# An encoder kernel: the sync engine's transfers in the order of the program

## The chip, the cores and the metric

The kernel runs on one core of one Trainium2 chip. A core has five engines with a queue of instructions each: TensorE (PE in the profile; PEld is its weight load), VectorE (DVE), ScalarE (ACT), GpSimd (POOL) and SyncE (SP). SP computes nothing here: it issues DMA transfers between HBM and the core's SBUF, one after the other, and an instruction in its queue that has to wait holds up all that stand behind it. The metric is the device time of one execution in microseconds (us).

## The reference

One layer of a bidirectional encoder on two sequences, 1024 and 256 tokens of 1024 features, in float32. After a norm, one projection feeds a Fourier mixing branch and a six-head latent attention; their outputs are joined and projected (`w_out`), then comes a SwiGLU feed-forward block with 2816 hidden units, and a last norm.

```python
def trunk(x):
    x = x + token_mixer(rms_norm(x, norm_mix_g), w_in, q_norm_g, w_q_up, kv_norm_g, w_kv_up, w_out)
    x = x + (silu(rms_norm(x, g) @ w_gate) * (rms_norm(x, g) @ w_up)) @ w_down
    return rms_norm(x, final_norm_g)
```

## The kernel before

**Arithmetic.** Each float32 operand is split into two parts, a rounded "hi" part and the rest "lo", and `mm3` (line 100) makes a product out of three: hi by hi, hi by lo, lo by hi. A weight therefore goes through four hands: SP loads it raw (`wload`, line 136, or `load_w`), ACT copies the hi part (line 93), POOL or DVE subtracts to get the lo part (line 98), and only then can TensorE use all of it. The raw weights share a pool of four buffers (`wraw`); a further load waits until POOL or DVE has read the oldest of them.

**Stages.** The token axis is cut into chunks of 512, 512 and 256 (`TC`). In order of time: the input projection, with the loads of `x` (`load_x`) and `w_in` (`load_w`); the query projections, whose results go to HBM through `q_rope` (line 589) and come back through `qload` (lines 695 and 697); the attention blocks (`Block`), in which the exponentials are turned by small transfers (`move`, line 808) and the row sums are stored (`inverse`, line 795) and read back spread out (`spread`, line 800); the output projection `out_proj`, which stores its result to `hd` (line 1106); the gate and up projections (`run`, `rest`, `prep`), eleven units of 256 hidden columns each, whose results go to HBM through `put` (line 1249); and the down projection (`down`), which reads them back by `load_a` (lines 1407 and 1409, five transfers a unit) and takes `w_down` through the class `Weights` (line 138). `load_h` (lines 1444, 1446) fetches the residual for the sum.

**What sets the order.** The kernel is written for a tile framework whose scheduler decides the order of each engine's queue. `tc.manual_schedule` names the engines whose queue keeps the order of the program instead: PE, ACT, DVE and POOL. SP is not among them, so the scheduler places SP's transfers by its own plan, and a load whose buffer is free may be put ahead of a store that the program issues earlier. Waits for data and for buffers are added by the framework.

**Around the two seams that matter below.** After the last attention head has started its last block, the program calls `inverse` for head 5, chunk 1 (a store of the row sums on SP that waits for DVE), and then `W.split(io + 2)`, which loads and splits the first two pieces of `w_out`:

```python
at(first[n] + 4, lambda: W.split(io + 2))
```

At the end of the gate and up stage the program goes through the last unit's `put`s, and then:

```python
load_a(0)
for t in range(3):
    split_a(0, t)
W.end = len(wspec)
W.split(idn + 2)
load_a(1)
```

`load_a(0)` reads what unit 0 left in HBM far earlier; `W.split(idn + 2)` loads four pieces of `w_down` and splits two. The down projection then runs units of two hidden tiles (`fp`) over three token chunks and eight output tiles (`m`); a group `down((fp,), m, t)` is 12 matmuls for a chunk of 512. PSUM has four buffers (`mm`) for these groups.

Of the kernel before, what the change touches and what calls it, by code (L numbers as in the profile page):

```python
# [35 lines left out]
def encoder_kernel(ctx, tc, A, out):  # L36
# [5 lines left out]
                mybir.EngineType.Activation,  # L42
                mybir.EngineType.DVE,
                mybir.EngineType.Pool,
            }
        )
    )
# [1595 lines left out]
```

## Time and profile before

| | |
|---|---|
| median of 3 runs | 1452.13 us (1449.49 to 1455.31) |
| the profiled execution, whole | 1450.82 us |
| its span, first to last instruction | 1449.0 us |
| DVE busy | 851.4 us (59%) |
| ACT busy | 548.7 us (38%) |
| POOL busy | 616.8 us (43%) |
| transfers on the hardware queue of SP (q1) | 150.74 MB, 34.0% of the 16 DMA engines' time |
| mean granted TensorE clock | 0.988 |

How to read it: times in the timeline are microseconds from the first instruction; a row of the timeline is a run of like instructions on one engine, with its start, its length and, in brackets, the idle time of the engine ahead of it and what ended that. `SPq` marks the issue of a transfer, not its flight; an `SPq` row is long when its later transfers had to wait.

### The profile page before, as it was taken

Reading aid. Unit: us, or ns where it says so; the run is one execution under the profiler, and the core shown is the slowest. Engines: PE = TensorE matmul, PEld = TensorE weight load, DVE = VectorE, ACT = ScalarE, POOL = GpSimd, SP = SyncE. Lnnn points to the kernel's source line nnn. Section 1 sums busy time; section 2 is a strip of 40 time slices with the busy share of each in tenths; the row PEclk is TensorE's granted clock in tenths of the full one; section 3 lists DMA queues with packets and bytes.
Section 4 is the critical chain, followed back from the end, with each engine's and each line's share of the span. In section 5 each row is a group of like instructions: output and inputs, shape, how many; then the busy total and the mean of one; then the engine's idle time right before and its main releaser. Section 6 shows DMA issues by size and latency. Waiting matters only on the chain.

```text
span 1449.0 us, 27553 instructions
## 1 busy us (share of the span) xinstructions
PE 1396.8 (96%) x11096; PEld 1350.2 (93%) x11096; DVE 851.4 (59%) x1291; ACT 548.7 (38%) x1107; POOL 616.8 (43%) x444
## 2 busy tenths in 40 slices
PE   9999998999989997899999999999999999999997
PEld 8999897888869997899999999999999999999996
DVE  6778668898993765954234324332432466777434
ACT  5554446676763424432222222222223332113133
POOL 3466524453542644264444444444353142334333
PEclk9999999999999998999999999999999999999998
DMA  7103445686765652031212121212222542234002
GB/s 256 58 1 121 148 131 141 154 203 152 198 187 145 205 159 75 16 110 66 65 60 95 57 69 67 95 49 73 70 84 89 174 164 89 85 128 161 1 37 110
DMA packets 76192, 157.50 MB, mean 109 GB/s; under 512 B 13216, under 2 KB 23200, under 8 KB 75936
## 3 DMA queue, kind: packets, MB, share of 16 engines
q1 hardware_dynamic: 73008, 150.74, 34.0%
q10 hardware_dynamic: 2736, 3.95, 0.8%
q8 instruction: 87, 1.43, 0.4%
q0 software_dynamic: 320, 1.05, 0.2%
q14 instruction: 41, 0.34, 0.1%
HBM read 99.57 MB, written 35.16 MB: 93 GB/s over the span
## 4 chain that ended last, share of the span: by engine, by line
PE 78%; DVE 10%; issue 3%; ACT 3%; POOL 2%; DMA 1%; SPq 0%; ACTq 0%; DVEq 0%; POOLq 0%
PE mm L112 49%; PE sc L112 22%; PE sc L747 1%; PE sc L748 1%; PE sc L751 1%; PE sc L750 1%; PE sc L749 1%; DVE mx L758 1%; DVE b L98 1%; DVE mx L98 1%; PE mm L824 1%; DVE c L1114 1%; POOL wo L98 0%; DVE at L98 0%; DVE wraw L818 0%
## 5 line engine op out<-in xcount | busy, mean ns | idle before, releaser
L112 PE MATMUL mm<-at,whl 128*128 128x256 f32 x2640 | 304.6, 278 | 4.2 <-DVE h L1437 2.3
L112 PEld LDWEIGHTS mm<-at,whl 128*128 128x128 f32 x2640 | 302.7, 189 | 5.4 <-DVE h L1437 2.9
L112 PE MATMUL sc<-b,wo 128*128 128x256 f32 x2288 | 291.2, 278 | 4.7 <-ACT wo L93 2.5
L112 PEld LDWEIGHTS sc<-b,wo 128*128 128x128 f32 x2288 | 275.0, 189 | 5.3 <-ACT wo L93 3.5
L98 POOL TENSOR_TENSOR wo<-wraw,wo 128x512 fp32r<-128x512 f32 x148 | 200.7, 1379 | 164.7 <-ACT wo L93 164.7
L1257 DVE TENSOR_TENSOR e<-e,sc 128x512 f32<-128x512 f32 x64 | 43.9, 688 | 225.6 <-PE sc L112 225.6
L1437 DVE TENSOR_TENSOR h<-h,mm 128x512 f32<-128x512 f32 (+1 forms) x192 | 111.8, 596 | 103.2 <-PE mm L112 102.6
L98 POOL TENSOR_TENSOR whl<-wraw,whl 128x1024 fp32r<-128x1024 f32 (+3 forms) x49 | 117.3, 2410 | 85.4 <-ACT whl L93 78.4
L112 PE MATMUL mm<-hn,wo 128*128 128x256 f32 x1056 | 130.7, 277 | 0.0
L112 PE MATMUL mm<-b,wo 128*128 128x256 f32 x1056 | 127.1, 276 | 0.7 <-ACT b L93 0.5
L112 PEld LDWEIGHTS mm<-hn,wo 128*128 128x128 f32 x1056 | 125.5, 188 | 0.0
L112 PEld LDWEIGHTS mm<-b,wo 128*128 128x128 f32 x1056 | 123.1, 188 | 1.1 <-ACT b L93 0.7
L112 PEld LDWEIGHTS mm<-mx,whl 128*128 128x128 f32 x960 | 114.3, 191 | 2.2 <-POOL whl L98 1.5
L112 PE MATMUL mm<-mx,whl 128*128 128x256 f32 x960 | 115.0, 281 | 1.1 <-POOL whl L98 0.9
L93 ACT ACTIVATE at<-araw 128x512 fp32r<-128x512 f32 x55 | 32.8, 624 | 160.0 <-DMA araw<-a 106.7
L93 ACT ACTIVATE wo<-wraw 128x512 fp32r<-128x512 f32 x156 | 87.8, 619 | 4.3 <-PE mm L112 2.0
L112 PE MATMUL mm<-pt,vt 128*128 128x512 f32 (+1 forms) x324 | 83.1, 391 | 6.2 <-DVE pt L98 5.8
L98 POOL TENSOR_TENSOR wo<-tmp,wo 128x512 fp32r<-128x512 f32 x22 | 29.3, 1335 | 137.7 <-ACT wo L93 137.7
L1450 POOL TENSOR_TENSOR h<-h,araw 128x512 f32<-128x512 f32 (+1 forms) x24 | 27.5, 1151 | 136.6 <-DVE h L1437 84.7
L98 POOL TENSOR_TENSOR pt<-wraw,pt 128x512 fp32r<-128x512 f32 x40 | 60.6, 1514 | 52.6 <-ACT pt L93 46.8
L1085 POOL TENSOR_TENSOR hacc<-hacc,tmp 128x512 f32<-128x512 f32 (+1 forms) x35 | 42.2, 1205 | 86.5 <-ACT tmp L1084 80.3
L112 PEld LDWEIGHTS mm<-pt,vt 128*128 128x128 f32 x324 | 57.2, 191 | 19.3 <-DVE pt L98 7.6
(199 smaller groups left out, 2269.7 us busy)
## 6 DMA issues: line engine op xcount, KB each, us to landing
Y<-P SPq DMA_DIRECT2D x160, 128.0 KB, 2.6
wraw<-in_w_gate SPq DMA_DIRECT2D x22, 512.0 KB, 4.2
wraw<-in_w_up SPq DMA_DIRECT2D x22, 512.0 KB, 4.3
wraw<-in_w_down SPq DMA_DIRECT2D x22, 512.0 KB, 3.5
araw<-a SPq DMA_DIRECT2D x44, 256.0 KB, 4.4
a<-e SPq DMA_DIRECT2D x42, 256.0 KB, 2.0
araw<-in_x SPq DMA_DIRECT2D x32, 256.0 KB, 4.4
wraw<-in_w_out SPq DMA_DIRECT2D x16, 512.0 KB, 4.0
```

Of the source, the lines that this page charges most:

```text
L93: nc.scalar.activation(o, i, AF.Copy)
L98: eng.tensor_tensor(o, i, f(hi), op=ALU.subtract)
L112: nc.tensor.matmul(o[:, c], L[a], R[b][:, c], start=first and i == 0 and j == 0, stop=end, skip_group_check=again)
L747: nc.tensor.matmul(o, qn[0][:, cs], k[0], start=True, stop=False)
L748: nc.tensor.matmul(o, qn[0][:, cs], k[1], start=False, stop=False)
L749: nc.tensor.matmul(o, qn[1][:, cs], k[0], start=False, stop=False)
L750: nc.tensor.matmul(o, qr[0][:, cs], krst[kt], start=False, stop=False)
L751: nc.tensor.matmul(o, qr[1][:, cs], krst[kt], start=False, stop=True)
L1085: nc.gpsimd.tensor_tensor(acc[t], acc[t], q, op=ALU.add)
L1257: add = lambda o, x, y: nc.vector.tensor_tensor(o, x, y, op=ALU.add)
L1437: nc.vector.tensor_tensor(hview(m, t), hview(m, t), o, op=ALU.add)
L1450: nc.gpsimd.tensor_tensor(HV[m, t], HV[m, t], hres.pop((m, t)), op=ALU.add)
```

## The change

SP joins the engines whose queue keeps the program's order. No transfer is added, taken away or resized, and the order of the four other engines stays what it was.

```diff
@@ -42,6 +42,7 @@
                 mybir.EngineType.Activation,
                 mybir.EngineType.DVE,
                 mybir.EngineType.Pool,
+                mybir.EngineType.SP,
             }
         )
     )
```

## The prediction

> **What bounds the kernel now.** I read the page's head first, then the timeline of SP against the order in which the source issues transfers, and then, at each place where the two differ, the engine that waits for the transfer.
>
> ```profile
> span 1449.0 us, 27553 instructions
> ...
> PE 1396.8 (96%) x11096; PEld 1350.2 (93%) x11096; DVE 851.4 (59%) x1291; ACT 548.7 (38%) x1107; POOL 616.8 (43%) x444
> ...
> L112 PE MATMUL mm<-at,whl 128*128 128x256 f32 x2640 | 304.6, 278 | 4.2 <-DVE h L1437 2.3
> ```
>
> TensorE is busy for 1396.8 of 1449.0 us, so at most 52 us can be won anywhere, and a transfer matters only where its lateness reaches TensorE. The third row is the down projection: TensorE stood idle ahead of it for 4.2 us in all. Now SP's queue where that stage begins:
>
> ```profile
> 1083.35 1.58 SPq L138 DMA_DIRECT2D wraw<-in_w_down  x2
> ...
> 1103.12 1.75 SPq L1407 DMA_DIRECT2D araw<-a  x4
> ...
> 1107.96 1.58 SPq L138 DMA_DIRECT2D wraw<-in_w_down  x2
> ...
> 1116.99 10.68 SPq L1249 DMA_DIRECT2D a<-e  x4
> ...
> 1128.74 0.32 SPq L1249 DMA_DIRECT2D b<-tmp  x1
> 1129.15 1.83 SPq L1407 DMA_DIRECT2D araw<-a  x4
> ...
> 1131.88 9.63 SPq L138 DMA_DIRECT2D wraw<-in_w_down  x4
> ```
>
> In the program the last unit's five `put`s (line 1249) come first, then `load_a(0)`, then four `w_down` loads, then `load_a(1)`. SP's own order is different: two `w_down` loads run 33 us ahead of those stores, `load_a(0)` 14 us, the next two `w_down` 9 us. That is a prefetch over the seam, and the change takes it away. The same kind of lead stands in four other places.
>
> **The change, part by part.** It adds and removes no instruction: it only moves transfers in one queue. Each load moves back behind the stores written ahead of it.
>
> *1. The seam to the down projection.* What the prefetch buys:
>
> ```profile
> 1108.40 2.72 ACT L93 ACTIVATE at<-araw 128x512 fp32r<-128x512 f32 x5
> ...
> 1111.03 1.99 ACT L93 ACTIVATE whl<-wraw 128x1024 fp32r<-128x1024 f32 x2
> ...
> 1112.15 4.75 POOL L98 TENSOR_TENSOR whl<-wraw,whl 128x1024 fp32r<-128x1024 f32 x2 [2.96 <-ACT whl L93]
> ...
> 1127.10 0.39 PE L112 MATMUL mm<-at,whl 128*128 128x256 f32 x2
> ...
> 1129.37 20.86 PE L112 MATMUL mm<-at,whl 128*128 128x256 f32 x167 [1.89 <-DVE at L98]
> ...
> 1131.93 0.63 ACT L93 ACTIVATE at<-araw 128x512 fp32r<-128x512 f32 x1 [18.91 <-DMA araw<-a]
> ...
> 1134.24 0.63 ACT L93 ACTIVATE at<-araw 128x512 fp32r<-128x512 f32 x1 [1.68 <-DMA araw<-a]
> ```
>
> Both weights were split by 1116.9, while TensorE still worked on the unit before, and it lost 1.89 us. Afterwards the last store, which waits for the stage's last result, still goes at 1128.74, and only then comes `load_a(0)`. Before, exactly there, stood `load_a(1)` and two `w_down` loads of the same sizes, so their flight is the measure; the rows are the issue views of 1129.1 to 1131.3 and of 1131.5 to 1133:
>
> ```profile
> araw<-a SPq DMA_DIRECT2D x4, 256.0 KB, 3.6
> araw<-b SPq DMA_DIRECT2D x1, 256.0 KB, 5.3
> ...
> wraw<-in_w_down SPq DMA_DIRECT2D x2, 512.0 KB, 6.2
> ```
>
> ACT got the first `a` at 1131.93 and the third at 1134.24; the fifth, `b`, issued at 1131.1, landed 5.3 later at 1136.4, ahead of the weights. The two `w_down`, issued at 1131.88 and 0.4 later, landed 6.2 us on in the median, the pair about 1.2 apart: 1137.7 and 1138.9. The hi copies (1.99 / 2 = 1.0 each) end at 1138.7 and 1139.9, POOL's lo parts (4.75 / 2 = 2.4 each, one after the other) at 1141.1 and 1143.5. The first group of 12 matmuls ends with those that need the second lo part: 1143.5 + 2 x 0.125 (20.86 / 167) = 1143.75. Before, two of the twelve had run and the other ten ended at 1129.37 + 10 x 0.125 = 1130.6. Loss: **13.1 us**, all of it on TensorE. Behind it nothing else is late: `load_a(1)` comes four 512 KB loads later, about 5 us, and the four PSUM buffers let TensorE run on for four groups (6 us) without DVE.
>
> The bounds: if the second lo part could be hidden, 2.4 less (10.7); if the flights of 6.2 grew by a half because more loads are queued at once, 3.1 more (16.2).
>
> A long gap also costs clock. The windows view (length; busy PE, PEld, DVE, ACT, POOL; granted clock; DMA):
>
> ```profile
> 561.00:570.00 9.00, 0.28 (x1) 0.28 (x1) 1.45 (x3) 1.59 (x3) 7.77 (x7) 0.65 0.08 29
> 570.00:572.00 2.00, 2.00 (x7) 1.47 (x8) 2.00 (x4) 1.75 (x4) 0.00 (x0) 0.50 0.00 0
> ...
> 574.00:576.00 2.00, 2.00 (x19) 2.00 (x18) 1.09 (x2) 1.39 (x4) 0.47 (x1) 1.00 0.00 0
> ...
> 1130.00:1140.00 10.00, 10.00 (x76) 10.00 (x76) 5.00 (x8) 4.73 (x7) 3.61 (x2) 0.83 0.73 253
> ```
>
> After 9 us with 0.28 of matmul the clock was 0.50 until about 574, some 4.2 us of work at half rate: 2.1 us. At the seam the small gap already cost 0.17 x 10 = 1.7. I add the difference, **0.4**, bounds 0 and 2.1 (a second slow stretch). The Trainium skill (TensorE: Matmul & The Clock Gate, What's actually happening) says that the clock halves after at least one idle window of about 3.4 us and is back after one busy one; the 4.2 us of half rate agree roughly, and by it both versions would pay 1.7 and the term would be 0.
>
> *2. The first two pieces of `w_out`.*
>
> ```profile
> 408.07 9.52 SPq L138 DMA_DIRECT2D wraw<-in_w_out  x3
> ...
> 421.40 2.01 ACT L93 ACTIVATE whl<-wraw 128x1024 fp32r<-128x1024 f32 x2
> ...
> 422.28 0.32 SPq L795 DMA_DIRECT2D rs<-rs  x1
> ...
> 422.54 5.16 POOL L98 TENSOR_TENSOR whl<-wraw,whl 128x1024 fp32r<-128x1024 f32 x2 [1.60 <-ACT whl L93]
> ...
> 422.67 5.58 DVE L98 TENSOR_TENSOR mx<-araw,mx 128x512 fp32r<-128x512 f32 x2
> ...
> 428.17 1.28 DVE L98 TENSOR_TENSOR pt<-mm,pt 128x512 fp32r<-128x512 f32 x2
> 428.91 1.97 PE L824 MATMUL mm<-ident,P 128*128 128x128 f32 x8 [3.67 <-DVE pt L98]
> ```
>
> ```profile
> wraw<-in_w_out SPq DMA_DIRECT2D x1, 512.0 KB, 3.6
> ```
>
> These loads move from 408.07 to behind the row-sum store at 422.28. The first is issued at 422.7 and lands at 426.3 (3.6, the issue view of the load at 421.56), the second about 1.2 later. ACT waits for the first from 421.40 and ends the two hi copies at 428.5 instead of 423.4: 5.1 late. Its next work, two hi copies of `pt`, feeds DVE's `pt`, which began at 428.17 before; now it can begin at 429.05, 0.9 late. So most of the 5.1 falls into the 3.67 us for which TensorE waited anyway. ACT's further copies are then about 1.4 behind. I take **1.5**, near the nearest row, with bounds 0.9 and 5.1.
>
> DVE was held there: its two `mx` subtractions took 5.58 beside POOL's two of 5.16. The Trainium skill (SBUF — State Buffer, SBUF: two separate sides) says that DVE instructions with two SBUF inputs and GpSimd instructions lock each other out of one port pair; this row agrees. By that rule POOL's later work leaves DVE free at 424 and touches only the next `mx` pair, and the term would be 0.9.
>
> *3. Loads that move and stay hidden.*
>
> ```profile
> 22.86 0.33 SPq L138 DMA_DIRECT2D wraw<-in_wkv  x1
> ```
>
> ```profile
> 108.53 1.78 ACT L93 ACTIVATE whl<-wraw 128x1024 fp32r<-128x1024 f32 x2
> ```
>
> ```profile
> 155.47 9.73 SPq L589 DMA_DIRECT2D qr<-qs  x12
> ```
>
> ```profile
> 164.14 1.06 ACT L93 ACTIVATE whl<-wraw 128x1024 fp32r<-128x1024 f32 x1 [0.44 <-ACT tmp L93]
> ```
>
> ```profile
> 542.43 0.33 SPq L1106 DMA_DIRECT2D hd<-h  x1
> ...
> 545.81 2.18 ACT L93 ACTIVATE wo<-wraw 128x512 fp32r<-128x512 f32 x4
> ...
> 552.53 0.42 DVE L1103 TENSOR_TENSOR hb<-mm,araw 128x256 f32<-128x256 f32 x1 [2.13 <-PE mm L112]
> ```
>
> `wkv` and the first `wq` pieces fall behind the last loads of `x`, but ACT splits them only at 108.53, some 50 us later. The first Fourier basis falls behind eight of the twelve query stores, to about 160, and lands at about 163.5; ACT wants it at 164.14, a margin under 1 us, and a miss would hit ACT alone. The four gate and up loads fall behind the store at 542.43. With the flight of 3.6 and 1.3 us for each further one, the first lands at 546.4 and the third at 549.0, so ACT ends its four copies at about 551 instead of 548.0; DVE follows and has 2.13 us idle ahead of 552.53. Cost 0; without that cover 2.8. Later `w_out` pieces are loaded two output tiles ahead of their split, and a tile's 48 matmuls last longer than a flight. In the attention stage `spread` and `move` change places with one row-sum store, and their users come six steps later (`LAG`).
>
> *4. What is won.* In the down projection SP stood with a `w_down` load that waited for POOL to free a buffer, and `load_a` and `load_h` behind it. In program order these come earlier and wait less. But TensorE's idle time there is 4.2 us in all, 1.9 of it at the seam. I take **-0.8**; bounds -2.3 (all the rest) and +2 (DVE and POOL meeting at new places).
>
> *Sum:* 13.1 + 0.4 + 1.5 - 0.8 = +14.2 us. The profiled execution took 1450.82 (span 1449.0, and 1.8 around it), which gives 1465.0; it is 1.3 below the median of 1452.13, to which the change is compared, so I forecast **1466 us**, +1.0%.
>
> **The rivals.**
> - *ACT's delay at 421 carries through whole, or the queued loads fly slower:* one of them adds 3.6 or 3.1 us, 1469 to 1470; both 1473. For it: ACT is in order and everything in the last head goes through it. Against: the 3.67 us of idle TensorE.
> - *A cheaper seam:* the weights come faster than the ones that followed `load_a(1)`, or POOL's first lo part starts earlier; 10.7 instead of 13.1, and 0.9 instead of 1.5 at `w_out`, give 1463, and 1461 if both clock and flight are kinder still.
> - *The other side, not slower:* the removed blocking decides. SP no longer stands in front of a full buffer pool; price: at most 2.3 us in the down stage, 1450. It decides only if the seam costs less than that, which needs the last stores issued some 11 us earlier than 1128.74, or the loads of `load_a(0)` to be let past a waiting store. Nothing in the rows shows SP passing a transfer that waits.
> - *The change does not bind:* the scheduler's order stays, 1452. The four engines already named do run in the source's order in the timeline, which speaks against it.
>
> **How the numbers follow.** Forecast 0.62 (1463 to 1468), dearer 0.22 (1468 to 1474), cheaper 0.09 (1459 to 1463), no change 0.04, other side 0.03. The range 1459 to 1474 takes in the bounds of the terms on both sides. About 0.5% (7.3 us) is what a measurement of this kernel can tell from no change: slower by more needs over 1459.4. That gives slower 0.92, same 0.06, faster 0.02.
>
> **What would show it.** In the profile after, `load_a(0)` right behind the line 1249 stores and the first `w_down` behind that; ACT idle before its first `at` and `whl`; a TensorE gap of 11 to 12 us before the down stage's matmuls and POOL's two lo parts just ahead of their flow; a granted clock of 0.5 in that stretch. At about 421 ACT waits some 5 us for `w_out`, with TensorE late by under 2. The gate and up stage between has its length unchanged. I am wrong if the seam's gap is under 8 us, or if a new gap stands elsewhere, above all at 560.

## The result and the profile after

The changed kernel took 1475.18 us (median of 4 runs, 1472.77 to 1478.01), the kernel before 1451.11 (4 runs beside it). The ratio is 1.0152, 95% interval 1.0128 to 1.0176: slower by 1.5%. The forecast was 1466, with a range that ended at 1474. The direction was right, and the time lies 1.2 us above the range.

The profiled execution of the changed kernel took 1472.77 us, 22.0 more than the one before. From its page: the span, the busy times of the engines, and the group of the down projection.

```profile
span 1471.0 us, 27548 instructions
...
PE 1399.8 (95%) x11096; PEld 1350.7 (92%) x11096; DVE 853.3 (58%) x1291; ACT 550.3 (37%) x1107; POOL 617.3 (42%) x444
...
L113 PE MATMUL mm<-at,whl 128*128 128x256 f32 x2640 | 308.1, 279 | 18.4 <-ACT whl L94 11.5
```

TensorE's busy time grew by 3.0 us and its idle time (span less busy) from 52.2 to 71.2; 14.2 of the 19.0 stand ahead of the down projection (18.4, 4.2 before). All lines of the source are one higher than before. Of the names in the rows, `at` and `whl` are the split parts of `a` and of a weight, `pt` and `mx` those of the turned exponentials and of the mixing branch's results, `araw` and `wraw` what was loaded, and `hacc` the running sum of squares of `h` for the norm.

TensorE runs the same 11096 instructions in the same order in both kernels, so the start of one instruction in both traces gives the lag at that point. Three rows of TensorE's timeline before, then four after: the first answers to the row at 428.91 that the prediction shows, the others to these three.

```profile
569.72 0.79 PE L188 MATMUL mm<-ssq,ones_r 128*128 128x512 f32 x1 [8.76 <-ACT ssq L93]
...
1301.00 2.20 PE L112 MATMUL mm<-at,whl 128*128 128x256 f32 x17 [0.84 <-DVE h L1437]
...
1348.80 1.42 PE L112 MATMUL mm<-at,whl 128*128 128x256 f32 x10 [1.29 <-DVE h L1437]
```

```profile
432.37 1.97 PE L825 MATMUL mm<-ident,P 128*128 128x128 f32 x8 [4.79 <-DVE pt L99]
...
573.87 0.80 PE L189 MATMUL mm<-ssq,ones_r 128*128 128x512 f32 x1 [11.62 <-ACT ssq L94]
...
1318.34 1.86 PE L113 MATMUL mm<-at,whl 128*128 128x256 f32 x14 [0.84 <-DVE h L1438]
...
1370.77 1.43 PE L113 MATMUL mm<-at,whl 128*128 128x256 f32 x10 [1.29 <-DVE h L1438]
```

The lag is 3.46 us at 428.91, 4.15 at 569.72, 17.34 at 1301.00 and 21.97 at 1348.80. Just ahead of the seam it is 4.00, by the last store on SP (1132.74 below, 1128.74 before). So the seam cost 13.3, where 13.5 was forecast; but the down stage, for which a gain of 0.8 was forecast, cost 4.6 more. The gap ahead of 570 grew by 2.86, from 8.76 to 11.62, where nothing was forecast; in the lag this shows as 0.7 only, because TensorE had run the stretch before at a quicker pace (last section). Ahead of 421 the lag wanders between -0.7 and +0.9 without a gap of TensorE that grew by more than 0.5; from 604 to the seam it stays at 4.00.

**The seam.** The rows are from the timelines of SP, ACT, POOL and TensorE after.

```profile
1132.74 0.32 SPq L1250 DMA_DIRECT2D b<-tmp  x1
1133.15 1.83 SPq L1408 DMA_DIRECT2D araw<-a  x4
...
1135.55 1.96 SPq L139 DMA_DIRECT2D wraw<-in_w_down  x4
...
1141.65 1.06 ACT L94 ACTIVATE whl<-wraw 128x1024 fp32r<-128x1024 f32 x1 [0.62 <-DMA wraw<-in_w_down]
...
1142.79 4.67 POOL L99 TENSOR_TENSOR whl<-wraw,whl 128x1024 fp32r<-128x1024 f32 x2 [29.60 <-ACT whl L94]
...
1142.76 1.22 PE L113 MATMUL mm<-at,whl 128*128 128x256 f32 x4 [11.50 <-ACT whl L94]
...
1147.51 4.75 PE L113 MATMUL mm<-at,whl 128*128 128x256 f32 x24 [0.67 <-POOL whl L99]
```

The chain is the one that was forecast, link by link: last store, five `a` loads, weights, ACT, POOL. POOL ends at 1142.79 + 4.67 = 1147.46; the forecast, 1143.5 plus that lag of 4.0, is 1147.5. The granted clock behind the gap was 0.50 from 1142 to 1150, as forecast (before: 0.59 and 0.55 in 1130 to 1134); what the clock alone cost was not measured apart from the chain.

**The first gate and up weights.** Rows of DVE, ACT and POOL after; below them those of DVE and POOL before.

```profile
547.99 0.68 DVE L99 TENSOR_TENSOR b<-c,b 128x512 fp32r<-128x512 f32 x1
...
549.98 0.63 ACT L94 ACTIVATE wo<-wraw 128x512 fp32r<-128x512 f32 x1 [2.15 <-DMA wraw<-in_w_gate]
552.68 1.68 ACT L94 ACTIVATE wo<-wraw 128x512 fp32r<-128x512 f32 x3 [2.07 <-DMA wraw<-in_w_up]
...
555.76 0.41 DVE L1104 TENSOR_TENSOR hb<-mm,araw 128x256 f32<-128x256 f32 x1
...
561.08 4.62 DVE L99 TENSOR_TENSOR wo<-wraw,wo 128x512 fp32r<-128x512 f32 x4
...
561.90 1.58 POOL L1217 TENSOR_TENSOR wraw<-wraw 128x512 f32<-128x512 f32 x1 [1.30 <-DVE wo L99]
...
571.90 1.26 POOL L1086 TENSOR_TENSOR hacc<-hacc,tmp 128x512 f32<-128x512 f32 x1
```

```profile
546.07 0.68 DVE L98 TENSOR_TENSOR b<-c,b 128x512 fp32r<-128x512 f32 x1
...
556.88 4.68 DVE L98 TENSOR_TENSOR wo<-wraw,wo 128x512 fp32r<-128x512 f32 x4
...
557.70 1.60 POOL L1216 TENSOR_TENSOR wraw<-wraw 128x512 f32<-128x512 f32 x1 [1.90 <-DVE wo L98]
...
567.75 1.26 POOL L1085 TENSOR_TENSOR hacc<-hacc,tmp 128x512 f32<-128x512 f32 x1
```

Ahead of this place DVE was 1.92 behind (547.99 against 546.07); what follows is counted beyond that. ACT stood before the weights for 2.15 and 2.07 us and ended its four copies 4.4 late (552.68 + 1.68 = 554.36, before 545.81 + 2.18 = 547.99). DVE's `h` and `hb`, which need none of these weights, came behind DVE's subtractions from them. DVE's idle time ahead of `hb` was used up, and `hb` still began 1.3 late (555.76, before 552.53). With it came late what stands behind it on DVE, up to the subtractions from the second pair of weights, which began 2.3 late. POOL's second operation of `sums0` waits for those: POOL was idle for 1.30 us ahead of it, as for 1.90 before. Eight operations of `sums0` stand ahead of the last `hacc`, and the gap of TensorE ends with that one (573.87). So the delay came through DVE's own queue: its slack was shorter than the delay.

**The down stage.** DVE, POOL and ACT in the last unit before the final one; first before, then after.

```profile
1334.55 2.49 DVE L98 TENSOR_TENSOR at<-araw,at 128x512 fp32r<-128x512 f32 x4
...
1337.14 4.77 POOL L98 TENSOR_TENSOR whl<-wraw,whl 128x1024 fp32r<-128x1024 f32 x2 [3.17 <-PE mm L112]
...
1335.43 0.63 ACT L93 ACTIVATE at<-araw 128x512 fp32r<-128x512 f32 x1 [1.22 <-DMA araw<-a]
```

```profile
1351.90 6.86 DVE L99 TENSOR_TENSOR at<-araw,at 128x512 fp32r<-128x512 f32 x4
...
1352.78 5.42 POOL L99 TENSOR_TENSOR whl<-wraw,whl 128x1024 fp32r<-128x1024 f32 x2 [1.47 <-PE mm L113]
...
1351.60 2.00 ACT L94 ACTIVATE whl<-wraw 128x1024 fp32r<-128x1024 f32 x2
...
1359.41 2.90 PE L113 MATMUL mm<-at,whl 128*128 128x256 f32 x12 [2.71 <-DVE h L1438]
```

Less the lag of 17.34, DVE began its four subtractions at the same time in both (1351.90 - 17.34 = 1334.56). Before, ACT still waited 1.22 us for an `a` tile that was late, so it split the weights later and POOL began at 1337.14, 0.10 after DVE's four had ended. After, the tile was there, ACT went on at once, POOL began 1.7 us earlier and met DVE: four subtractions took 6.86 instead of 2.49, the evacuations of PSUM behind them were late, and TensorE had no free bank for 2.71 us and then ran slowly (granted clock 0.62 in 1359 to 1361, 0.53 in the two after). Here the removed wait had been keeping two engines apart.

### The profile page after: what moved, and what is told of

It is laid out like the page before. It is cut to its first block, busy times and chain, and to the rows that moved or that the text cites. A ratio compares the mean times of both kernels' runs of the same rounds, so it can differ in the third digit from the quotient of the medians.

```text
span 1471.0 us, 27548 instructions
## 1 busy us (share of the span) xinstructions
PE 1399.8 (95%) x11096; PEld 1350.7 (92%) x11096; DVE 853.3 (58%) x1291; ACT 550.3 (37%) x1107; POOL 617.3 (42%) x444
## 3 DMA queue, kind: packets, MB, share of 16 engines
q8 instruction: 87, 1.43, 0.4%
## 4 chain that ended last, share of the span: by engine, by line
PE 74%; DVE 10%; issue 3%; DMA 2%; ACT 2%; POOL 2%; SPq 2%; ACTq 0%; DVEq 0%; POOLq 0%
PE mm L113 47%; PE sc L113 21%; PE sc L748 1%; PE sc L749 1%; PE sc L752 1%; PE sc L751 1%; PE sc L750 1%; DVE b L99 1%; SPq L809 1%; DVE mx L759 1%; DVE pt L99 1%; PE mm L825 1%; DVE c L1115 1%; DVE at L99 1%; POOL wo L99 1%
## 5 line engine op out<-in xcount | busy, mean ns | idle before, releaser
L113 PE MATMUL mm<-at,whl 128*128 128x256 f32 x2640 | 308.1, 279 | 18.4 <-ACT whl L94 11.5
```

The source lines that it names most:

```text
L113: nc.tensor.matmul(o[:, c], L[a], R[b][:, c], start=first and i == 0 and j == 0, stop=end, skip_group_check=again)
```

## The experiments

Most undo one part of the change in the changed kernel, by issuing some transfers elsewhere in the program; the last three also move work of POOL and ACT. SP keeps program order throughout. Times are medians; the kernel before took 1449.8 beside them.

**e_seam: the transfers of the seam early.** `load_a` is defined ahead of the loop, and:

```diff
     for n in range(14, len(seq)):
         prep(n + 6)
+        if n == len(seq) - 6:
+            W.end = len(wspec)
+            W.load(idn + 2)
+            load_a(0)
+            W.load(idn + 4)
         run(n)
...
-    load_a(0)
     for t in range(3):
         split_a(0, t)
-    W.end = len(wspec)
     W.split(idn + 2)
```

> The changed kernel, with the transfers of the seam issued earlier in the program: two w_down loads, load_a(0) and two more w_down loads stand ahead of the last unit's stores, which is the order that the scheduler had chosen there; nothing else differs. My theory: the gap of 11.50 us ahead of the down projection is the flight of these loads plus ACT's and POOL's splits, so it falls to about 2 us and the time by 13, from 1475.2 to about 1462. Rival: the loads only wait for their place among the other transfers, and the gap stays above 8 us; about 1473. Second rival: the gap of 2.71 us late in the down stage (near 1357) is a consequence of the seam's delay and goes with it; then about 1457.

Measured: 1461.09 us (6 runs, 1457.57 to 1465.19), ratio 1.0077 [1.0057, 1.0096]. TensorE's timeline at the seam and late in the down stage:

```profile
1131.31 8.96 PE L113 MATMUL mm<-at,whl 128*128 128x256 f32 x62 [1.88 <-DVE at L99]
...
1344.01 2.23 PE L113 MATMUL mm<-at,whl 128*128 128x256 f32 x9 [2.71 <-DVE h L1443]
```

The gap is 1.88 instead of 11.50, and TensorE's lag falls by 13.3 at this place. The first theory holds. The gap of 2.71 is still there, so it has a cause of its own.

**e_gate: the first gate and up weights early.**

```diff
         W.split(min(io + 8 + m + 3, idn))
+        if m in (4, 5):
+            load_pair(m - 4)
         if m == 6:
...
-        if m == 5:
-            load_pair(0)
-            load_pair(1)
```

> The changed kernel, with the first pair of w_gate loads issued one output tile earlier and the first pair of w_up loads ahead of the store of that tile and not behind it. My theory: in the changed kernel ACT stood before these weights for 2.15 and 2.07 us, DVE and POOL followed, and TensorE's gap at 562 grew from 8.76 to 11.62; the gap goes back to about 8.8, the one at 607 from 1.58 to about 0.5, and the time falls by 3.9 to about 1471. Rival: the delay at 562 was handed down from the late w_out pieces at 421, and the gap stays at 11.6; 1475.

Measured: 1473.91 (5 runs, 1471.77 to 1481.56), ratio 1.0175 [1.0151, 1.0199].

```profile
550.33 0.68 DVE L99 TENSOR_TENSOR b<-c,b 128x512 fp32r<-128x512 f32 x1
...
573.64 0.80 PE L189 MATMUL mm<-ssq,ones_r 128*128 128x512 f32 x1 [9.05 <-ACT ssq L94]
```

The gap falls by 2.57, from 11.62 to 9.05, with the delay at `w_out` still in place: it was not handed down. TensorE resumes only 0.23 earlier than in the changed kernel, because in this execution everything was already 2.34 later ahead of the loads: DVE's `b`, at 547.99 there, starts at 550.33. From this row to the end of the gap it is 25.88 us in the changed kernel and 23.31 in e_gate, again 2.57 less; before it was 23.65. The time alone could not have shown 2.6 us among runs that differ by ten; the row does. One part of the expectation failed: the gap at 607 stayed at 1.53. The loads did not cause it; the last section returns to it.

**e_wout: the first two pieces of `w_out` early.**

```diff
+                at(first[n] + 3, lambda: W.load(io + 2))
                 at(first[n] + 4, lambda: W.split(io + 2))
```

> The changed kernel, with the first two w_out loads issued one attention step earlier, ahead of the row-sum store. My theory: ACT no longer waits for them; TensorE's gap at 427 goes from 4.79 to about 3.7, and with it the stretch at half clock ahead of it; the time falls by 2.8 to about 1472.4. Rival: the half clock at 424 to 427 falls by chance and not with the gap; then it falls by 1.2 to 1474. Second rival: DVE's subtractions of mx again run beside POOL's lo parts of these weights (5.58 us for two in the kernel before, 1.29 in the changed one), and the gap stays above 4.5.

Measured: 1473.83 (6 runs, 1468.26 to 1480.29), ratio 1.017 [1.0146, 1.0195]. To compare three kernels here I take the time from DVE's pair of `pt` subtractions, just ahead of all this, to the matmul with which TensorE resumes. The first of these rows before, after and in e_wout:

```profile
421.42 0.74 DVE L98 TENSOR_TENSOR pt<-mm,pt 128x256 fp32r<-128x256 f32 x2
```

```profile
422.31 0.74 DVE L99 TENSOR_TENSOR pt<-mm,pt 128x256 fp32r<-128x256 f32 x2
...
423.58 1.81 SPq L139 DMA_DIRECT2D wraw<-in_w_out  x4
...
428.86 2.25 ACT L94 ACTIVATE whl<-wraw 128x1024 fp32r<-128x1024 f32 x2 [6.44 <-DMA wraw<-in_w_out]
...
423.56 1.29 DVE L99 TENSOR_TENSOR mx<-araw,mx 128x512 fp32r<-128x512 f32 x2
```

```profile
425.49 0.74 DVE L99 TENSOR_TENSOR pt<-mm,pt 128x256 fp32r<-128x256 f32 x2
...
426.74 5.59 DVE L99 TENSOR_TENSOR mx<-araw,mx 128x512 fp32r<-128x512 f32 x2
...
432.98 1.31 PE L825 MATMUL mm<-ident,P 128*128 128x128 f32 x7 [2.13 <-DVE pt L99]
```

428.91 - 421.42 = 7.49 before, 432.37 - 422.31 = 10.06 after, 432.98 - 425.49 = 7.49 in e_wout. So the late loads cost 2.57, and early ones give exactly that back. The gap itself misleads: it is 3.67 before and 2.13 in e_wout with the same end, because the matmuls ahead of it ran slower; the stretch at half clock, which was to go with the gap, stayed (granted clock 0.50 in 428 to 430). The second rival had half a point. DVE's `mx` pair is back beside POOL at 5.59; in the changed kernel it took 1.29, for POOL's weights were not there yet. So before the change TensorE waited for that meeting, and afterwards for the loads.

**e_down: the last `load_a` and `load_h` behind two `w_down` loads.**

```diff
-                if m == 1 and t == 1 and final:
-                    load_a(fp + 3)
                 if final and t == 1 and m == 5 or final and t == 2 and m == 2:
                     W.split(idn + 2 * fp + 4 + 2 * t)
-                if t == 1 and m == 4:
+                if m == 5 and t == 1 and final:
+                    load_a(fp + 3)
+                if t == 1 and m == (5 if final else 4):
                     load_h(fp)
```

> The changed kernel, with the last load_a and the last load_h issued behind two w_down loads and not ahead of them, as the scheduler had it; they land later. My theory: in the changed kernel these a tiles came early, ACT went on to split two w_down pieces 1.7 us sooner, and POOL's lo parts of them fell beside DVE's four at subtractions, which took 6.86 us where they took 2.49 before; TensorE then waited 2.71 us and ran at half clock behind it. Later loads keep the two apart: the four subtractions take about 2.5, the gap near 1357 goes, and the time falls by 4.9 to about 1470.3. Rival: DVE was slow because transfers wrote to SBUF beside it; then the later loads, which come nearer to the subtractions, leave them at 5 us or more and the gap stays; 1475. Second rival: the four take 2.5 again, but DVE and POOL meet elsewhere; a gap of 2 us or more at another place of the stage, 1474.

Measured: 1472.38 (5 runs, 1469.39 to 1475.15), ratio 1.0154 [1.0132, 1.0176].

```profile
1355.93 2.50 DVE L99 TENSOR_TENSOR at<-araw,at 128x512 fp32r<-128x512 f32 x4
...
1358.37 4.76 POOL L99 TENSOR_TENSOR whl<-wraw,whl 128x1024 fp32r<-128x1024 f32 x2 [3.02 <-PE mm L113]
...
1349.80 16.37 PE L113 MATMUL mm<-at,whl 128*128 128x256 f32 x143
```

POOL begins as DVE's four end, they take 2.50, and TensorE runs through. From DVE's four subtractions (1351.90 in the changed kernel, 1355.93 here) to the matmuls behind TensorE's next gap of 1.29 us it is 18.87 us in the changed kernel (to 1370.77) and 14.25 in e_down (to 1370.18), as in the kernel before: 4.6 us are won. ACT's last `a` tile again came late, by 1.11; the profile puts this wait down to TensorE, though in the changed kernel no wait stood there. Transfers that landed nearer to the subtractions did not slow them, so that rival falls: later loads made the kernel quicker here.

**e_seam_a and e_seam_w: half of the seam.** e_seam_a issues only `load_a(0)` early, e_seam_w only the four `w_down` loads; otherwise as e_seam.

> The changed kernel, with load_a(0) alone issued ahead of the last unit's stores; the first four w_down loads stay behind them. By the chain that I read at the seam (last store, five a loads, then the weights, ACT, POOL) the weights end last; their issue moves up by the 2.3 us of the a loads, so the gap of 11.50 falls only to about 9.2. Rival: the a tiles were what came last, and the gap falls below 5.

> The changed kernel, with the first four w_down loads alone issued ahead of the last unit's stores; load_a(0) stays behind them. POOL's lo parts are then long done; the third a load was split on DVE by 1138.7 in the changed kernel, 7.4 us after the gap's begin at 1131.3, so a gap of about 7.4 is left, and no second and third gap behind it (1.21 and 0.67). If both halves hold, neither early load alone brings even half of the 13 us. Rival: with the weights there the gap falls to about 2.

Measured: 1467.85 and 1477.35, one run each. The gap is 6.78 in e_seam_a and 9.54 in e_seam_w; both numbers missed the expectation, in opposite directions. First e_seam_a, then e_seam_w:

```profile
1132.22 1.83 SPq L139 DMA_DIRECT2D wraw<-in_w_down  x4
...
1135.99 1.06 ACT L94 ACTIVATE whl<-wraw 128x1024 fp32r<-128x1024 f32 x1 [21.81 <-DMA wraw<-in_w_down]
...
1137.10 1.22 PE L113 MATMUL mm<-at,whl 128*128 128x256 f32 x4 [6.78 <-ACT whl L94]
```

```profile
1141.36 1.99 ACT L94 ACTIVATE whl<-wraw 128x1024 fp32r<-128x1024 f32 x2
...
1142.45 1.22 PE L113 MATMUL mm<-at,whl 128*128 128x256 f32 x4 [9.54 <-ACT whl L94]
```

In e_seam_a the weights reached ACT 3.8 us after their issue (1132.22 to 1135.99), in the changed kernel 6.1 (1135.55 to 1141.65). Early `a` loads thus won the 2.4 us of their place in the queue and 2.3 of flight. In e_seam_w I had forgotten ACT's order: the program splits `a` before the weights, so weights that had long landed still waited for ACT until 1141.36, and POOL's lo parts followed. Neither early load alone brings half of the 13 us, as expected, but for a reason of its own each time.

**e_all: the four edits together.** e_seam, e_gate, e_wout and e_down in one kernel.

> The four edits of the runs before in one kernel: seam, gate and up, w_out, and the last load_a and load_h. My theory: the four places are all that the new order costs, and they add up: by the steps read off TensorE's timeline 13.3 + 2.4 + 2.5 + 4.5 = 22.7, so 1475.2 falls to about 1452.5, the time of the kernel before. Rival: the places compensate each other (the medians of the single runs give only 14.1 + 1.3 + 1.4 + 2.8 = 19.6), and 1455.6 is left, 0.3% above the kernel before. Second rival: there is a fifth place, and 1457 or more is left.

Measured: 1451.03 (12 runs, 1447.57 to 1457.38), ratio to the kernel before 1.0012 [0.9992, 1.0032]. The loss is back, 24.15 us by the medians. No fifth place shows: the interval leaves room for 4.6 us (0.0032 x 1449.8) at most.

**e_all_pool: POOL's sums behind the last `hacc`.** On top of e_all:

```diff
             prep(8)
-            sums0(0)
-            sums0(1)
...
             hch[1].pre()
+            sums0(0)
+            sums0(1)
             for k in range(4, 8):
                 parts0(k)
```

> The kernel with the four edits, and POOL's eight operations that form sums of the first gate and up weights (sums0) placed behind the last addition to hacc and not ahead of it. In the kernel before, that addition stood behind them at 567.75, though its input was there at 562.9, and TensorE's gap of 8.76 us ended with it. My theory: the addition comes 4.8 us earlier, the gap falls to about 4 and the time by 4.8 to 6 (a shorter stretch at half clock), to about 1447. Rival: the sums are wanted at once afterwards, and the gaps at 611 to 615 (2.5 and 1.6) grow by what is won; no change against the four edits.

Measured: 1447.16 (12 runs, 1443.86 to 1452.86), ratio to the kernel before 0.9981 [0.9963, 0.9998].

```profile
559.00 0.49 PE L189 MATMUL mm<-ssq,ones_r 128*128 128x512 f32 x1 [1.07 <-ACT ssq L94]
...
572.73 0.53 PE L189 MATMUL mm<-ssq,ones_r 128*128 128x256 f32 x1 [3.63 <-ACT ssq L94]
```

The gap shrinks from 9.07 (e_all) to 1.07, more than expected, but part is given back: the next chunk's addition to `hacc` now stands behind the sums, and gaps of 3.63 and 1.43 are new. Some 4 us remain (1451.03 to 1447.16), less than the 4.8 to 6 expected, and the gaps that the rival named did not grow. It confirms which order on POOL set the gap at 562, and it is the fastest version found, 0.2% ahead of the kernel before, with an interval that ends just below 1.

**e_all_pool_w5 and e_w5: the split of `w_out` one step later**, on top of e_all_pool and alone in the changed kernel.

```diff
-                at(first[n] + 4, lambda: W.split(io + 2))
+                at(first[n] + 5, lambda: W.split(io + 2))
```

> The kernel with the four edits and the sums behind hacc, and the split of the first two w_out pieces one attention step later than in all other kernels (their loads stay early). In the four-edit kernel DVE's two subtractions of mx took 5.58 us beside POOL's two lo parts of w_out (5.15), where they take 1.29 alone, and TensorE resumed 1.3 us behind them. My theory: one step later POOL's lo parts run beside DVE work that reads PSUM, which was not slowed in the changed kernel (1.29 for two pt subtractions beside POOL's 4.69), so the mx pair takes 1.3, TensorE resumes 2 to 4 us sooner and the time falls by as much, from 1447.2 to about 1444. Rival: the pieces are then late for the first output tile at about 440, or they meet the next mx pair; no gain, 1447 or more.

> The changed kernel with that later split alone, the w_out loads still behind the row-sum store. My theory: ACT no longer stands 6.44 us before the first piece with the pt copies behind it; TensorE's resumption at 432.4 comes about 3 us sooner, as far as before the change or beyond it. Rival: ACT waits for the piece one step later all the same, and the delay only moves behind 432; the first matmul on w_out (445 in the changed kernel) starts no sooner.

Measured: 1449.21 (12 runs), ratio 0.999 [0.9975, 1.0005], no gain; and 1477.85, one run. In e_all_pool_w5 the rival came true:

```profile
428.54 4.41 DVE L99 TENSOR_TENSOR mx<-araw,mx 128x512 fp32r<-128x512 f32 x2
```

The first `mx` pair was free (1.29), and POOL met the next one, which took 4.41; TensorE waited 3.63 behind it. In e_w5 TensorE resumed at 428.53 and then waited 3.01 at 431.4; the first matmul on `w_out` came at 442.41 instead of 444.09. Taken from DVE's `pt` pair (423.34 here), the way to that matmul is 19.07 us, where the changed kernel needs 21.78 and the kernel before 19.00. So by this one trace nearly the whole loss at this place was won back without moving a load; one run at 1477.85 says nothing of it.

## Why the prediction was right or wrong

| step | predicted | lag in the two profiles | undone alone |
|---|---|---|---|
| 1, seam, with the clock term | +13.5 | +13.3 | 13.3 (e_seam) |
| 2, first two `w_out` pieces | +1.5 | +2.6 | 2.6 (e_wout) |
| 3, gate and up weights | 0 | +0.7 (gap +2.86, less the pace) | 2.6 (e_gate) |
| 4, down stage | -0.8 | +4.6 | 4.6 (e_down) |

*Step 1 was right* in mechanism and size, down to the moment at which POOL's second lo part ends. The flight was 6.1 where 6.2 had been taken. The row chosen there, loads with the same neighbours in the queue, is why it fitted.

*Step 2 was right in its mechanism and mis-sized in one term.* The flight was taken as 3.6, from a single load at a quiet moment; right behind the row-sum store the first took 428.86 - 423.58 = 5.3. The two hi copies ended at 431.1 instead of 428.5, moved by the lag of 0.9 to 429.4: 1.7 later. The forecast's ACT chain then gives 1.7 more than the 0.9 that was its nearest row: 2.6, as measured. That four loads were issued together is not the reason for the 5.3 (last section). DVE's `mx` pair did run free of POOL (1.29 instead of 5.58), but ACT's delay set the time, so the 0.9 that counted on the free pair did not come.

*Step 3 failed in the size of the delay, and so in the cover.* ACT was to be 3.0 late (551 against 548.0), covered by the 2.13 us for which DVE was idle ahead of 552.53. Even by these numbers 0.9 was left, and the cost was not 0. ACT was 4.4 late: counted from the issue of the first load (545.09), the first reached it after 4.9 us (549.98) and the third after 7.6 (552.68), where 3.6 and 6.2 had been taken. DVE's idle time was used, `hb` came 1.3 late, and behind it DVE's `b`, beside POOL, took 2.94 instead of 2.39; so the subtractions that POOL's sums wait for came 2.3 late, and TensorE's 8.76 us gap with them. The price without cover was given as 2.8 and e_gate measured 2.6; that they are close is luck, for the delay was longer and the cover was there. The prediction named 560 as the place where it would be wrong, and it was.

*Step 4 failed in its sign.* "In program order these come earlier and wait less" holds: the last `a` loads went out 12.8 us earlier (1334.29 less the lag of 17.34, against 1329.70). But I counted only what the waiting cost, 2.3 at most, and not what it kept apart. The bound of +2 for "DVE and POOL meeting at new places" named the mechanism and had no row under it: the meeting at 421 in the kernel before (5.58 for two subtractions, 1.29 alone) prices such a meeting at 4.3 us; here it cost 6.86 - 2.49 = 4.4.

The Trainium skill (SBUF — State Buffer, SBUF: two separate sides) says that a DVE instruction with two SBUF inputs and a GpSimd instruction exclude each other from a shared port pair, whichever starts first holding it to its end. The runs agree: beside POOL, `at` and `mx` subtractions with two SBUF inputs took 6.86 for four and 5.59 or 4.41 for two, and evacuations from PSUM stayed at 0.6 to 0.7 each. I had weighed this rule at `w_out` only, and not at every place where a load moves against POOL's work.

The sum came out too low by the two failed steps, 2.6 and 5.4, and by 1.1 for step 2. Undone alone, the four places give 13.3 + 2.6 + 2.6 + 4.6 = 23.1, where 14.2 was forecast and the change cost 22.0 in the two profiles and 24.1 by the medians. The dearer rival did not hold it either: it put the excess into ACT's delay at 421 and slower flights at the seam, and these came out at 1.1 and at nothing.

## What to carry to other kernels

When one queue's order changes, write down for each moved load which engine comes free earlier or later, and follow that engine's queue to the next thing for which TensorE waits. Idle time on the way covers a delay only up to its own length, so set the two numbers beside each other; and read a flight off a load that has the same neighbours in the queue as the moved one will have. A wait that disappears can cost time, if it happened to keep two engines off a shared resource: look for pairs of rows that end and begin within a fraction of a microsecond. When comparing traces, compare when the bottleneck resumes, not how long its gap is.

## What the runs showed that I had not expected

**Two paces of TensorE at one granted clock.** Windows of 140 us in the down stage, first e_all_pool, then e_all_pool_w5, which run the same code there (length; busy time of TensorE, its weight loads, DVE, ACT, POOL; granted clock; DMA):

```profile
1130.00:1270.00 140.00, 139.83 (x1234) 139.63 (x1233) 90.13 (x138) 35.44 (x54) 45.01 (x28) 1.00 0.39 132
```

```profile
1130.00:1270.00 140.00, 140.00 (x1191) 140.00 (x1191) 85.25 (x134) 37.64 (x57) 44.67 (x27) 1.00 0.38 129
```

One matmul took 139.83 / 1234 = 113 ns or 140 / 1191 = 118 ns, 4% more, both at a granted clock of 1.00. The stretches at the slow pace lie elsewhere in each execution; in the second row they cost some 5 us (43 matmuls fewer). Both profiles hold all 11096 matmuls. This hides or imitates changes of a few microseconds in a single time: between the rows at 432 and 562 it gave the changed kernel 2.2 us. It also goes with the gap at 607, which was 0.48 or 0.49 in the four profiles with the slow pace ahead of it (before, e_down, e_all, e_seam_w) and 1.53 to 1.58 in the six with the quick one (after, e_seam, e_gate, e_wout, e_seam_a, e_w5): there TensorE waits for ACT's `b`, and whatever it gains it waits. What sets the pace stays open; no run here was made to tell.

**The flight of 512 KB** from issue to ACT was 3.8 us right behind a store of 256 KB (e_seam_a), 6.1 behind five loads of 256 KB, and 5.3 right behind the 2 KB store of the row sums. The first and the last were each the first of four loads, so the number issued together does not make the difference. In e_wout and e_all only two loads stand behind the row-sum store, and they landed 5.4 us after their issue in the median; the 3.6 of the prediction belongs to a load that went out just ahead of that store. In the changed kernel the DMA engines moved 2 GB/s from 424 to 425 and nothing from 425 to 426. Why a load waits behind so small a store stays open.
